# Sums of weight blocks made by adding transfers, loads begun earlier, and a new order of seven products

## The chip, the cores and the metric

The kernel runs on one core of one Trainium2 chip. The metric is the device time in microseconds (us), as the median of several executions. One more execution was profiled; all rows below come from it.

## The reference, cut to what matters

Two layers of a decoder trunk on 256 tokens of width 1024. Each layer is an FFN, a token mixer and a second FFN, each with a residual:

```
x = x + 0.5 * swiglu(rms(x), w_up, w_down)     # four times in all
x = x + mixer(rms(x))                          # delta/retention heads, then dilated/differential attention

def swiglu(h, w_up, w_down):                   # w_up: 1024 x 5632, w_down: 2816 x 1024
    gate, up = split(h @ w_up, 2)
    return (silu(gate) * up) @ w_down
```

All of it is float32. The change touches the four FFNs only.

## The kernel before, in words

**Numbers and products.** Each float32 weight block `w` is split into `hi` (ScalarE, line 219) and `lo = w - hi` (VectorE, called DVE, line 220), and each product is made of three matmuls on TensorE (PE): lines 321, 322 and 323. Blocks are 128 x 1024 elements, 512 KB.

**The stream.** `stream` lists all weight blocks in the order in which PE uses them. `block()` hands out the next one and keeps four more in preparation (`LOOKAHEAD`), by calling `feed()`, which issues the load of a plain block into a `w` tile on the queue of SP (line 218, five buffers) and emits lines 219 and 220 into five `hi` and five `lo` buffers.

**The up half of an FFN.** The 2816 columns are done in six chunks (0 to 4 of 512 columns, 5 of 256), each for gate and for up. Chunk 0 and chunk 5 are plain: 8 and 4 blocks of 12 matmuls. Chunks 1 and 2, and 3 and 4, form pairs (`seven_and`): the second of a pair (`mate`) is plain, with blocks G0 to G3 and U0 to U3, and for the first a 2 x 2 block product of Strassen's kind with seven products P1 to P7 replaces the eight (gate and up columns against the two halves of the contraction). Let W00, W01, W10, W11 be the four quarters of the weight: first index the half of the rows, second gate or up. Each quarter comes in two blocks (p = 0, 1). The sums of weights are:

```
a = W00 (P1)          t = W00 + W01 (P5)      d = W11 (P3)
u = t + W11 (P6)      b = W01 + W11 (P7)      c = W10 (P2)      u + W10 (P4)
```

A product block takes 6 matmuls. The raw quarters and the sums live in tiles with the tag `raw`, ten buffers (`RAW_BUFS`), and so does `xf`, two tiles that `sums` needs while it makes the sums of the inputs (`forms`: `keep`, then `fhP` and `flP`, lines 404, 411, 275, 276). In `form` the DVE makes t, u, b and u + W10 by adds of 128 x 1024 (line 180).

**The down half.** `seven_down` makes the product of the first eight row blocks for both column halves in the same way, mixed with the plain blocks H0 to H6; seven plain blocks for the second half follow. Here the loads are `early`: begun eight blocks ahead in place of four, and t and b are made by two transfers into the same tile, the second of them with `accum_op=ALU.add`, issued by GpSimd (POOL, line 172). u and u + W10 are made by DVE.

**What sets the order.** Each engine works through its own queue in order. The instructions are put on the queues ahead of time by a scheduler that mostly follows the order in which they are written. A tile of a tag waits until one of its buffers is free. Small steps of other work (`sums`, `turn`) are mixed in by `tick()` after each block.

Of the kernel before, what the change touches and what calls it, by code (L numbers as in the profile page):

```python
# [15 lines left out]
ALU = mybir.AluOpType  # L16
# [9 lines left out]
KF = FF // P  # L26
# [6 lines left out]
W_BUFS = 5  # L33
S_BUFS = 5
LOOKAHEAD = 4
LEAD, EARLY, RAW_BUFS = 4, 8, 10
GDN_STEPS, RET_STEPS, GDN_LAG = 2, 3, 2
LAMBDA_INIT = 0.8 - 0.6 * math.exp(-0.3)
BIG = 1.0e30
# [6 lines left out]
def trunk(ctx, tc, a, out):  # L46
# [34 lines left out]
                r.append((kk, n, pieces))  # L81
        return r

    SEVEN = ("P1", "G0", "G1", "P6", "G2", "G3", "P7", "U0", "U1", "P5", "U2", "U3", "P2", "P4", "P3")

    DOWN = ("H0", "H1", "P1", "H2", "P6", "H3", "P7", "H4", "P5", "P2", "H5", "P4", "P3", "H6")

    def one(w, k0, nk, c, n=CW):
        return (k0, nk, n, [(w, c, n)])

    def seven(w, cols, n, order, early=False, **between):

        kb = BLK // n

        def quarter(i, j, p):
            r0 = (4 * i + kb * p) * P
            return w[r0:r0 + kb * P, cols[j]:cols[j] + n].rearrange("(k p) c -> p k c", p=P)

        st = {}
        r = []  # L100
        for x in order:
            if x[0] == "P":
                r += [(x, p, st, quarter, n, early) for p in range(4 // kb)]
            else:
                r.append(between[x[0]][int(x[1])])
        return r
# [21 lines left out]

    def down_runs(w):

        return seven(w, (0, CW), CW, DOWN, True, H=cut([one(w, 8, KF - 8, 0)])) + cut([one(w, 8, KF - 8, CW)])

    def in0_runs(w):
        r = [one(w, 0, 8, 512), one(w, 0, 8, 0), one(w, 0, 8, 2048, 264), one(w, 0, 8, 1024),
# [7 lines left out]
    def out_runs(w, first):  # L142
        return [one(w, k0, 4, c * CW) for k0 in (first, 4 - first) for c in (0, 1)]

    stream = (up_runs(a["l0_ffn1_w_up"], True) + down_runs(a["l0_ffn1_w_down"])
              + cut(in0_runs(a["l0_w_in"]) + out_runs(a["l0_w_out"], 4))
              + up_runs(a["l0_ffn2_w_up"]) + down_runs(a["l0_ffn2_w_down"])
              + up_runs(a["l1_ffn1_w_up"]) + down_runs(a["l1_ffn1_w_down"])
              + cut(in1_runs(a["l1_w_in"]) + out_runs(a["l1_w_out"], 4))
              + up_runs(a["l1_ffn2_w_up"]) + down_runs(a["l1_ffn2_w_down"]))  # L150

    ready = []
    pos = [0, 0]
# [1 line left out]
    spool = [None]  # L155
    loaded = [0]

    def load(x, p, st, quarter, n, early):

        def raw(nm):  # L160
            if nm not in st:
                st[nm] = spool[0].tile([P, BLK], F32, tag="raw", name="raw", bufs=RAW_BUFS)
            return st[nm]

        if early:

            for nm, *src in {"P1": (("a", (0, 0)),), "P6": (("t", (0, 1), (0, 0)), ("d", (1, 1))),
                             "P7": (("b", (0, 1), (1, 1)),), "P2": (("c", (1, 0)),)}.get(x, ()):
                v = raw(nm + str(p)).rearrange("p (k n) -> p k n", n=n)
                nc.sync.dma_start(out=v, in_=quarter(*src[0], p))  # L170
                if src[1:]:
                    nc.gpsimd.dma_start(out=v, in_=quarter(*src[1], p), accum_op=ALU.add)
            return
        for nm, i, j in {"P1": (("a", 0, 0),), "P6": (("b", 0, 1), ("d", 1, 1)), "P2": (("c", 1, 0),)}.get(x, ()):
            nc.sync.dma_start(out=raw(nm + str(p)).rearrange("p (k n) -> p k n", n=n), in_=quarter(i, j, p))

    def form(x, p, st, early):

        def add(out, in0, in1):
            nc.vector.tensor_tensor(out=out, in0=in0, in1=in1, op=ALU.add)  # L180

        def new():
            return spool[0].tile([P, BLK], F32, tag="raw", name="raw", bufs=RAW_BUFS)

        g = {k[0]: v for k, v in st.items() if k[1] == str(p)}
        if x == "P6":
            if not early:
                st[f"t{p}"] = g["t"] = new()
                add(g["t"], g["a"], g["b"])
            st[f"u{p}"] = g["u"] = new()  # L190
            add(g["u"], g["t"], g["d"])
        elif x == "P7" and not early:
            add(g["b"], g["b"], g["d"])
        elif x == "P4":
            add(g["u"], g["u"], g["c"])
        return g[{"P1": "a", "P6": "u", "P7": "b", "P5": "t", "P2": "c", "P4": "u", "P3": "d"}[x]]

    def feed():
        i = pos[1]
        while loaded[0] < len(stream) and loaded[0] <= i + (EARLY if stream[loaded[0]][-1] is True else LEAD):  # L200
            if isinstance(stream[loaded[0]][0], str):
                if spool[0] is None:
                    break
                load(*stream[loaded[0]])
            loaded[0] += 1
        pos[1] += 1
        hi = wpool.tile([P, BLK], F32R, tag="hi", name=f"hi{i}", bufs=S_BUFS)
        lo = wpool.tile([P, BLK], F32R, tag="lo", name=f"lo{i}", bufs=S_BUFS)
        if isinstance(stream[i][0], str):
            n = stream[i][4]  # L210
            k = BLK // n
            w = form(*stream[i][:3], stream[i][5])
        else:
            k, n, pieces = stream[i]
            w = wpool.tile([P, BLK], F32, tag="w", name=f"w{i}", bufs=W_BUFS)
            wv = w[:, :k * n].rearrange("p (k n) -> p k n", n=n)
            for at, m, src in pieces:
                nc.sync.dma_start(out=wv[:, :, at:at + m], in_=src)
        nc.scalar.copy(out=hi[:, :k * n], in_=w[:, :k * n])  # L219
        nc.vector.tensor_tensor(out=lo[:, :k * n], in0=w[:, :k * n], in1=hi[:, :k * n].bitcast(F32), op=ALU.subtract)  # L220
        ready.append((k, hi[:, :k * n].rearrange("p (k n) -> p k n", n=n),
                      lo[:, :k * n].rearrange("p (k n) -> p k n", n=n)))

# [165 lines left out]
    def ffn(n, nxt):  # L389
        with tc.tile_pool(name="gpool", bufs=1) as gpool:  # L390
# [5 lines left out]
            def sums(src_hi, src_lo):  # L396
# [9 lines left out]
                    yield  # L406
                q = {(i, t): xf[i][:, :, t * P:(t + 1) * P] for i in range(2) for t in range(NT)}
                keep = gpool.tile([P, 4, P], F32, tag="post", name="keep", bufs=4)
                for nm, i0, i1, op in (("P7", q[0, 0], q[0, 1], ALU.subtract), ("P5", q[0, 1], q[1, 1], ALU.subtract),
                                       ("P6", None, q[0, 0], ALU.subtract), ("P3", None, q[1, 0], ALU.add)):  # L410
                    nc.vector.tensor_tensor(out=keep, in0=keep if i0 is None else i0, in1=i1, op=op)
                    hi = gpool.tile([P, 4, P], F32R, tag="fh" + nm, name="fh" + nm)
                    lo = gpool.tile([P, 4, P], F32R, tag="fl" + nm, name="fl" + nm)
                    split(hi, lo, keep)
                    forms[nm] = (hi, lo)
                    yield
# [44 lines left out]
            def seven_and(c, mate):  # L461


                pa, pb, pc, pd = pA("p1"), pB("p6"), pA("p5"), pA("p7")
                gate = [pA("gate"), pB("gate")]
                product("P1", pa)
                q = post("q")
                nc.scalar.copy(out=q, in_=pa)
                xs_run(gate, xT_hi, xT_lo, 0, 4)
                product("P6", pb)  # L470
                tt(q, q, pb)
                xs_run(gate, xT_hi, xT_lo, 4, 4)
                s2 = [silu(gate[t], t) for t in range(NT)]
                product("P7", pd)
                r = post("r")
                tt(r, q, pd)
                up = [pB("up"), pA("up")]
                xs_run(up, xT_hi, xT_lo, 0, 4)
                product("P5", pc)
                tt(r, pc, r, ALU.subtract)  # L480
                xs_run(up, xT_hi, xT_lo, 4, 4)
                next(spawn(turn(mate, [times(up[t], s2[t], t) for t in range(NT)], CW)))
                product("P2", pa, True)
                s0 = silu(pa, 0)
                product("P4", pd, True)
                g1 = post("g1")
                tt(g1, q, pd)
                s1 = silu(g1, 1)
                product("P3", pc, True)
                tt(q, pc, q, ALU.subtract)  # L490
                next(spawn(turn(c, [times(q, s0, 0), times(r, s1, 1)], CW)))

            spool[0] = gpool
            c = 0
# [17 lines left out]
            def seven_down(y):  # L512
# [19 lines left out]
                product("P6", pb)  # L532
                tt(q, q, pb)
                rest(1)
                product("P7", pd)
                r = post("r")
                tt(r, q, pd)
                rest(1)
                into(1, 0, q, 0.5)
                into(0, 1, q, -0.5)  # L540
                product("P5", pc)
                tt(r, pc, r, ALU.subtract)
                product("P2", pa, True)
                into(0, 0, pa, 0.5)
                rest(1)
                into(1, 1, r, 0.5)
                product("P4", pd, True)
                into(1, 0, pd, 0.5)
                product("P3", pc, True)
                into(0, 1, pc, 0.5)  # L550
                rest(1)

            for hf in range(2):
# [8 lines left out]
                g = spawn(half_done(y, hf, 0.5, nxt))  # L562
                next(g, None)
            spool[0] = None

    def out_proj(oT_hi, oT_lo, nxt, first, need):
        ys = [[pA(f"y{h}") for _ in range(NT)] for h in range(2)]
# [759 lines left out]
```

## Time and profile before

| | us |
|---|---|
| three timed runs, median | 1010.08 |
| lowest, highest | 1007.51, 1011.33 |
| profiled execution, its own time | 1007.63 |
| its span, first to last instruction | 1005.8 |
| PE busy | 985.9 (98%) |
| DVE busy | 880.1 (88%) |

The span is what the profile shows from the first to the last instruction; the time of the execution has 1.8 us more around it. PE matmuls are pipelined, so that one of 390 ns starts every 227 ns; busy shares of PE are high whatever it does, and starts are the better measure.

### The profile page before, as it was taken

The numbers are of one execution on the slowest core, as the hardware profiler recorded it, in microseconds if no ns is written. First come the engines' busy times: TensorE is split into PE (matmuls) and PEld (weight loads), VectorE is DVE, ScalarE is ACT, GpSimd is POOL, SyncE is SP. The second block draws the span as 40 slices with busy tenths as digits, with TensorE's granted clock in tenths as the row PEclk, the third lists the DMA queues.
The fourth block names the chain that finished last, engine by engine and source line by source line (L and its number), as shares of the span: only waits on it lengthen the run. The fifth ranks groups of instructions, "written<-read, shape, count | busy, mean of one in ns | idle before, by whom it ended". The sixth has DMA issues, their size and how long they took to land.

```text
span 1005.8 us, 13951 instructions
## 1 busy us (share of the span) xinstructions
PE 985.9 (98%) x5076; PEld 812.9 (81%) x5076; DVE 880.1 (88%) x1191; ACT 609.0 (61%) x829; POOL 48.9 (5%) x56
## 2 busy tenths in 40 slices
PE   7999999999999999999999999999999999999997
PEld 6788878888777888888788888878877888888785
DVE  6999999679997699999979899998679879999994
ACT  6576666579543566666656566656556556666562
POOL 0000100100001000000000000100100000001000
PEclk9999999999999999999999999999999999999999
DMA  9665963765403577499267747935752566749731
GB/s 321 228 228 180 291 200 128 238 171 149 141 12 110 156 259 245 124 277 267 84 212 270 248 144 241 292 101 188 232 168 88 167 210 209 248 150 289 230 106 62
DMA packets 104708, 192.69 MB, mean 192 GB/s; under 512 B 6560, under 2 KB 16944, under 8 KB 104640
## 3 DMA queue, kind: packets, MB, share of 16 engines
q1 hardware_dynamic: 98752, 179.89, 55.1%
q0 software_dynamic: 5312, 11.30, 5.6%
q8 instruction: 40, 0.66, 0.3%
q10 hardware_dynamic: 576, 0.61, 0.2%
q14 instruction: 28, 0.23, 0.1%
HBM read 190.73 MB, written 1.05 MB: 191 GB/s over the span
## 4 chain that ended last, share of the span: by engine, by line
PE 89%; DVE 5%; ACT 2%; issue 1%; DMA 1%; POOL 1%; SPq 0%; POOLq 0%; ACTq 0%; DVEq 0%
PE p L322 7%; PE p L323 7%; PE p L321 7%; PE y L321 6%; PE y L323 6%; PE y L322 6%; PE gate L323 6%; PE gate L321 6%; PE gate L322 6%; PE up L321 4%; PE up L322 4%; PE up L323 4%; PE ca L321 2%; PE ca L322 2%; PE ca L323 2%; PE gtr L452 2%
## 5 line engine op out<-in xcount | busy, mean ns | idle before, releaser
L220 DVE TENSOR_TENSOR lo<-w,hi 128x1024 fp32r<-128x1024 f32 (+2 forms) x238 | 284.5, 1210 | 65.0 <-ACT hi L219 64.6
L219 ACT CAST hi<-w 128x1024 fp32r<-128x1024 f32 (+2 forms) x238 | 245.5, 1044 | 128.7 <-PE y L323 50.7
L219 ACT CAST hi<-raw 128x1024 fp32r<-128x1024 f32 x168 | 174.4, 1053 | 132.2 <-DVE raw L180 49.5
L220 DVE TENSOR_TENSOR lo<-raw,hi 128x1024 fp32r<-128x1024 f32 x168 | 201.6, 1218 | 15.4 <-ACT hi L219 14.0
L321 PE MATMUL gate<-hi,xT_hi 128*128 128x512 f32 x256 | 101.3, 400 | 2.1 <-ACT xT_hi L278 1.9
L323 PE MATMUL gate<-hi,xT_lo 128*128 128x512 f32 x256 | 101.0, 395 | 0.0
L322 PE MATMUL gate<-lo,xT_hi 128*128 128x512 f32 x256 | 100.7, 393 | 0.0
L180 DVE TENSOR_TENSOR raw<-raw 128x1024 f32<-128x1024 f32 x80 | 97.0, 1216 | 0.3
L321 PE MATMUL y<-hi,gT_hi 128*128 128x512 f32 x224 | 87.2, 392 | 1.8 <-ACT hi L219 1.8
L323 PE MATMUL y<-hi,gT_lo 128*128 128x512 f32 x224 | 87.4, 390 | 0.0
L322 PE MATMUL y<-lo,gT_hi 128*128 128x512 f32 x224 | 87.2, 389 | 0.0
L321 PE MATMUL p<-hi,fhP 128*128 128x512 f32 x192 | 75.2, 392 | 0.2
L322 PE MATMUL p<-lo,fhP 128*128 128x512 f32 x192 | 74.9, 390 | 0.1
L323 PE MATMUL p<-hi,flP 128*128 128x512 f32 x192 | 74.7, 389 | 0.0
L321 PE MATMUL up<-hi,xT_hi 128*128 128x512 f32 x192 | 74.7, 389 | 0.0
L322 PE MATMUL up<-lo,xT_hi 128*128 128x512 f32 x192 | 74.7, 389 | 0.0
L323 PE MATMUL up<-hi,xT_lo 128*128 128x512 f32 x192 | 74.7, 389 | 0.0
L321 PEld LDWEIGHTS gate<-hi,xT_hi 128*128 128x128 f32 x256 | 48.5, 190 | 12.3 <-ACT xT_hi L278 2.3
L323 PEld LDWEIGHTS gate<-hi,xT_lo 128*128 128x128 f32 x256 | 48.6, 190 | 10.3
L322 PEld LDWEIGHTS gate<-lo,xT_hi 128*128 128x128 f32 x256 | 48.7, 190 | 9.7
L321 PEld LDWEIGHTS y<-hi,gT_hi 128*128 128x128 f32 x224 | 41.7, 188 | 11.2 <-ACT hi L219 3.0
L323 PEld LDWEIGHTS y<-hi,gT_lo 128*128 128x128 f32 x224 | 42.1, 188 | 8.7
(322 smaller groups left out, 1868.0 us busy)
## 6 DMA issues: line engine op xcount, KB each, us to landing
w<-l_ffn_w_up SPq DMA_DIRECT2D x95, 512.0 KB, 4.2
raw<-l_ffn_w_up SPq DMA_DIRECT2D x64, 512.0 KB, 4.9
w<-l_ffn_w_down SPq DMA_DIRECT2D x56, 512.0 KB, 5.1
w<-l_w_in SPq DMA_DIRECT2D x50, 512.0 KB, 3.8
raw<-l_ffn_w_down SPq DMA_DIRECT2D x40, 512.0 KB, 6.5
w<-l_ffn_w_up SPq DMA_DIRECT2D x34, 256.0 KB, 4.8
raw<-l_ffn_w_down POOLq DMA_DIRECT2D x16, 512.0 KB, 9.9
w<-l_w_out SPq DMA_DIRECT2D x16, 512.0 KB, 3.6
```

The costliest lines, as they stand in the source:

```text
L180: nc.vector.tensor_tensor(out=out, in0=in0, in1=in1, op=ALU.add)
L219: nc.scalar.copy(out=hi[:, :k * n], in_=w[:, :k * n])
L220: nc.vector.tensor_tensor(out=lo[:, :k * n], in0=w[:, :k * n], in1=hi[:, :k * n].bitcast(F32), op=ALU.subtract)
L321: nc.tensor.matmul(ps, lhsT=xh, rhs=wh, start=start, stop=False, skip_group_check=more)
L322: nc.tensor.matmul(ps, lhsT=xh, rhs=wl, start=False, stop=False, skip_group_check=more)
L323: nc.tensor.matmul(ps, lhsT=xl, rhs=wh, start=False, stop=stop, skip_group_check=more)
L452: nc.tensor.transpose(ps[:, j * P:(j + 1) * P], gs[t][:, j * P:(j + 1) * P], ident)
```

## The change

Up and down parts now share one way of loading and one order of products. t and b are made by adding transfers in all parts. After `hi` and `lo` of P6 are made from u, an adding transfer from GpSimd puts W10 on top of u, and P4 takes it as it is. u itself is still an add of DVE (t + d). Loads of raw blocks begin eight blocks ahead everywhere, at most two stream entries of that kind in one `feed`, after the `w` load of that `feed` and not before it, and none of the next FFN's before it has begun. The order of products is P1, P6, P5, P3, P7, P2, P4; the input sums are made in the order P5, P6, P3, P7, and the code that combines the products follows: `r = P5 - q`, then `u0 = P3 - q`, then `r = r - P7`, then P2, and at last `q = q + P4` (P2 still adds onto P1's bank, P3 onto P5's, P4 onto P7's).

```
-LEAD, EARLY, RAW_BUFS = 4, 8, 10
+LEAD, RAW_BUFS = 8, 10
-    SEVEN = ("P1", "G0", "G1", "P6", "G2", "G3", "P7", "U0", "U1", "P5", "U2", "U3", "P2", "P4", "P3")
+    SEVEN = ("P1", "G0", "G1", "P6", "G2", "G3", "P5", "U0", "U1", "P3", "P7", "U2", "U3", "P2", "P4")
-    DOWN = ("H0", "H1", "P1", "H2", "P6", "H3", "P7", "H4", "P5", "P2", "H5", "P4", "P3", "H6")
+    DOWN = ("H0", "H1", "P1", "H2", "P6", "H3", "P5", "H4", "P3", "P7", "H5", "P2", "P4", "H6")
...
     def load(x, p, st, quarter, n):
-        if early:
...
-        for nm, i, j in {"P1": (("a", 0, 0),), "P6": (("b", 0, 1), ("d", 1, 1)), "P2": (("c", 1, 0),)}.get(x, ()):
-            nc.sync.dma_start(out=raw(nm + str(p)).rearrange("p (k n) -> p k n", n=n), in_=quarter(i, j, p))
+        for nm, *src in {"P1": (("a", (0, 0)),), "P6": (("t", (0, 1), (0, 0)), ("d", (1, 1))),
+                         "P7": (("b", (0, 1), (1, 1)),), "P2": (("c", (1, 0)),)}.get(x, ()):
+            v = raw(nm + str(p)).rearrange("p (k n) -> p k n", n=n)
+            nc.sync.dma_start(out=v, in_=quarter(*src[0], p))
+            if src[1:]:
+                nc.gpsimd.dma_start(out=v, in_=quarter(*src[1], p), accum_op=ALU.add)
...
         if x == "P6":
-            if not early:
-                st[f"t{p}"] = g["t"] = new()
-                add(g["t"], g["a"], g["b"])
             st[f"u{p}"] = g["u"] = new()
-            add(g["u"], g["t"], g["d"])
-        elif x == "P7" and not early:
-            add(g["b"], g["b"], g["d"])
-        elif x == "P4":
-            add(g["u"], g["u"], g["c"])
+            nc.vector.tensor_tensor(out=g["u"], in0=g["t"], in1=g["d"], op=ALU.add)
...
     def feed():
-        while loaded[0] < len(stream) and loaded[0] <= i + (EARLY if stream[loaded[0]][-1] is True else LEAD):
...
+        some = 0
+        while loaded[0] < len(stream) and loaded[0] <= i + LEAD:
+            if isinstance(stream[loaded[0]][0], str):
+                if spool[0] is None or loaded[0] >= ends[0] or some == 2:
+                    break
+                some += 1
+                load(*stream[loaded[0]])
+            loaded[0] += 1
...
+        if stream[i][0] == "P6":
+            nc.gpsimd.dma_start(out=w.rearrange("p (k n) -> p k n", n=n), in_=stream[i][3](1, 0, stream[i][1]),
+                                accum_op=ALU.add)
```

## Rows read from the trace of the kernel before

**Rows 1.** The page, busy times, and busy tenths in 40 slices

```profile
PE 985.9 (98%) x5076; PEld 812.9 (81%) x5076; DVE 880.1 (88%) x1191; ACT 609.0 (61%) x829; POOL 48.9 (5%) x56
...
DVE  6999999679997699999979899998679879999994
```

**Rows 2.** Timeline of PE, second FFN (start us, us, instruction), and the chain

```profile
350.04 0.39 PE L321 MATMUL gate<-hi,xT_hi 128*128 128x512 f32 x1
...
352.53 0.40 PE L323 MATMUL gate<-hi,xT_lo 128*128 128x512 f32 x1
...
375.61 0.87 PE gtr L452 x8
```

**Rows 3.** Second FFN (length; busy PE, PEld, DVE, ACT, POOL; clock; DMA; GB/s)

```profile
350.04:528.40 178.36, 177.86 (x813) 147.20 (x812) 165.31 (x183) 110.70 (x136) 6.47 (x5) 1.00 0.67 210
```

**Rows 4.** Waits of PE in all (us in total, times, longest)

```profile
PE y L321 <- ACT hi L219: 1.8, 4, 0.4
```

**Rows 5.** Timeline of PE at the start of a down half, second FFN

```profile
482.27 0.39 PE L323 MATMUL p<-hi,flP 128*128 128x512 f32 x1
...
483.65 0.73 PE L321 MATMUL y<-hi,gT_hi 128*128 128x512 f32 x2 [0.44 <-ACT hi L219]
...
484.23 0.39 PE L322 MATMUL p<-lo,fhP 128*128 128x512 f32 x1
```

**Rows 6.** Timeline of DVE and ScalarE at the same place

```profile
477.48 0.68 DVE L411 TENSOR_TENSOR keep<-keep,xf 128x512 f32<-128x512 f32 x1
...
479.57 0.69 DVE L411 TENSOR_TENSOR keep<-keep,xf 128x512 f32<-128x512 f32 x1
...
480.29 1.23 DVE L180 TENSOR_TENSOR raw<-raw 128x1024 f32<-128x1024 f32 x1
...
481.61 1.05 ACT L219 CAST hi<-raw 128x1024 fp32r<-128x1024 f32 x1 [0.69 <-DVE raw L180]
```

**Rows 7.** Waits of SP's queue

```profile
SPq L170 <- DVE keep L411: 20.3, 4, 5.1
```

**Rows 8.** The chain in the first FFN (start us, us, what)

```profile
37.87 2.27 DVE raw L180 x2
```

**Rows 9.** Timeline of PE there

```profile
44.55 0.39 PE L321 MATMUL p<-hi,fhP 128*128 128x512 f32 x1
...
46.27 0.39 PE L323 MATMUL p<-hi,flP 128*128 128x512 f32 x1
```

**Rows 10.** Line 180 over the span (duration ns min/median/max)

```profile
L180 DVE TENSOR_TENSOR raw<-raw x80: 1208/1215/1226, 33.6 to 968.5; 128x1024 f32<-128x1024 f32 x80
```

**Rows 11.** Two saturated stretches: plain loads alone, and both kinds

```profile
8.00:14.00 6.00, 5.57 (x14) 4.31 (x15) 5.21 (x8) 5.17 (x13) 0.00 (x0) 1.00 1.05 406
...
642.00:646.00 4.00, 4.00 (x23) 3.38 (x22) 4.00 (x6) 2.02 (x3) 0.00 (x0) 1.00 1.10 263
```

**Rows 12.** The first pair of the second FFN as a stretch

```profile
372.73:415.50 42.77, 42.77 (x198) 35.59 (x197) 40.60 (x42) 27.20 (x31) 0.00 (x0) 1.00 0.59 196
```

**Rows 13.** Line 172 over the span (ns min/median/max), and us to landing

```profile
L172 POOL DMA_DIRECT2D raw<-l_ffn_w_down x16: 1195/1197/1402, 106.4 to 927.7; - x16
...
DMA to landing us min/median/max: 6.3/9.9/11.9
```

**Rows 14.** DMA issues (KB each, median us to landing)

```profile
raw<-l_ffn_w_up SPq DMA_DIRECT2D x64, 512.0 KB, 4.9
```

**Rows 15.** Timeline of DVE in the first pair of the second FFN

```profile
375.46 3.49 DVE L180 TENSOR_TENSOR raw<-raw 128x1024 f32<-128x1024 f32 x3
...
380.12 1.23 DVE L220 TENSOR_TENSOR lo<-raw,hi 128x1024 fp32r<-128x1024 f32 x1
```

**Rows 16.** Timeline of PE and DVE around a read of P6

```profile
427.37 0.39 PE L323 MATMUL p<-hi,flP 128*128 128x512 f32 x1
...
429.28 1.22 DVE L180 TENSOR_TENSOR raw<-raw 128x1024 f32<-128x1024 f32 x1
...
430.41 0.68 DVE L432 TENSOR_TENSOR q<-q,p 128x512 f32<-128x512 f32 x1
```

More of the change, by code (lines that the diff above doesn't have):

```diff
@@ L82, in cut, with seven @@
         return r
-    SEVEN = ("P1", "G0", "G1", "P6", "G2", "G3", "P7", "U0", "U1", "P5", "U2", "U3", "P2", "P4", "P3")
-    DOWN = ("H0", "H1", "P1", "H2", "P6", "H3", "P7", "H4", "P5", "P2", "H5", "P4", "P3", "H6")
+    SEVEN = ("P1", "G0", "G1", "P6", "G2", "G3", "P5", "U0", "U1", "P3", "P7", "U2", "U3", "P2", "P4")
+    DOWN = ("H0", "H1", "P1", "H2", "P6", "H3", "P5", "H4", "P3", "P7", "H5", "P2", "P4", "H6")
     def one(w, k0, nk, c, n=CW):
         return (k0, nk, n, [(w, c, n)])
-    def seven(w, cols, n, order, early=False, **between):
+    def seven(w, cols, n, order, **between):
         kb = BLK // n
@@ L102, in seven @@
             if x[0] == "P":
-                r += [(x, p, st, quarter, n, early) for p in range(4 // kb)]
+                r += [(x, p, st, quarter, n) for p in range(4 // kb)]
             else:
@@ L129, in down_runs @@
     def down_runs(w):
-        return seven(w, (0, CW), CW, DOWN, True, H=cut([one(w, 8, KF - 8, 0)])) + cut([one(w, 8, KF - 8, CW)])
+        return seven(w, (0, CW), CW, DOWN, H=cut([one(w, 8, KF - 8, 0)])) + cut([one(w, 8, KF - 8, CW)])
     def in0_runs(w):
@@ L143, in out_runs @@
         return [one(w, k0, 4, c * CW) for k0 in (first, 4 - first) for c in (0, 1)]
[L145 to L150, printed above, removed]
+    stream, ends = [], []
+    for l, w_in, w_out, in_runs, out_first in ((0, a["l0_w_in"], a["l0_w_out"], in0_runs, 4),
+                                               (1, a["l1_w_in"], a["l1_w_out"], in1_runs, 4)):
+        for f in (1, 2):
+            stream += up_runs(a[f"l{l}_ffn{f}_w_up"], not stream) + down_runs(a[f"l{l}_ffn{f}_w_down"])
+            ends.append(len(stream))
+            if f == 1:
+                stream += cut(in_runs(w_in) + out_runs(w_out, out_first))
     ready = []
@@ L156, in trunk, with load @@
     loaded = [0]
-    def load(x, p, st, quarter, n, early):
+    def load(x, p, st, quarter, n):
         def raw(nm):
@@ L163, in raw, with form @@
             return st[nm]
-        if early:
[L167 to L173, printed above, removed]
-        for nm, i, j in {"P1": (("a", 0, 0),), "P6": (("b", 0, 1), ("d", 1, 1)), "P2": (("c", 1, 0),)}.get(x, ()):
-            nc.sync.dma_start(out=raw(nm + str(p)).rearrange("p (k n) -> p k n", n=n), in_=quarter(i, j, p))
-    def form(x, p, st, early):
-        def add(out, in0, in1):
-            nc.vector.tensor_tensor(out=out, in0=in0, in1=in1, op=ALU.add)
+        for nm, *src in {"P1": (("a", (0, 0)),), "P6": (("t", (0, 1), (0, 0)), ("d", (1, 1))),
[4 more added lines that the diff above has]
+                nc.gpsimd.dma_start(out=v, in_=quarter(*src[1], p), accum_op=ALU.add)
+    def form(x, p, st):
         def new():
@@ L199, in feed @@
         i = pos[1]
-        while loaded[0] < len(stream) and loaded[0] <= i + (EARLY if stream[loaded[0]][-1] is True else LEAD):
[L201 to L205, printed above, removed]
         pos[1] += 1
@@ L208, in feed @@
         lo = wpool.tile([P, BLK], F32R, tag="lo", name=f"lo{i}", bufs=S_BUFS)
[L209 to L213, printed above, removed]
+        w = None
+        if not isinstance(stream[i][0], str):
             k, n, pieces = stream[i]
@@ L218, in feed @@
                 nc.sync.dma_start(out=wv[:, :, at:at + m], in_=src)
+        some = 0
[6 more added lines that the diff above has]
+            loaded[0] += 1
+        if w is None:
+            n = stream[i][4]
+            k = BLK // n
+            w = form(*stream[i][:3])
         nc.scalar.copy(out=hi[:, :k * n], in_=w[:, :k * n])
         nc.vector.tensor_tensor(out=lo[:, :k * n], in0=w[:, :k * n], in1=hi[:, :k * n].bitcast(F32), op=ALU.subtract)
+        if stream[i][0] == "P6":
+            nc.gpsimd.dma_start(out=w.rearrange("p (k n) -> p k n", n=n), in_=stream[i][3](1, 0, stream[i][1]),
+                                accum_op=ALU.add)
         ready.append((k, hi[:, :k * n].rearrange("p (k n) -> p k n", n=n),
@@ L408, in sums @@
                 keep = gpool.tile([P, 4, P], F32, tag="post", name="keep", bufs=4)
-                for nm, i0, i1, op in (("P7", q[0, 0], q[0, 1], ALU.subtract), ("P5", q[0, 1], q[1, 1], ALU.subtract),
-                                       ("P6", None, q[0, 0], ALU.subtract), ("P3", None, q[1, 0], ALU.add)):
+                for nm, i0, i1, op in (("P5", q[0, 1], q[1, 1], ALU.subtract), ("P6", None, q[0, 0], ALU.subtract),
+                                       ("P3", None, q[1, 0], ALU.add), ("P7", q[0, 0], q[0, 1], ALU.subtract)):
                     nc.vector.tensor_tensor(out=keep, in0=keep if i0 is None else i0, in1=i1, op=op)
@@ L473, in seven_and @@
                 s2 = [silu(gate[t], t) for t in range(NT)]
-                product("P7", pd)
+                product("P5", pc)
                 r = post("r")
-                tt(r, q, pd)
+                tt(r, pc, q, ALU.subtract)
                 up = [pB("up"), pA("up")]
                 xs_run(up, xT_hi, xT_lo, 0, 4)
-                product("P5", pc)
-                tt(r, pc, r, ALU.subtract)
+                product("P3", pc, True)
+                u0 = post("u0")
+                tt(u0, pc, q, ALU.subtract)
+                product("P7", pd)
+                tt(r, r, pd, ALU.subtract)
                 xs_run(up, xT_hi, xT_lo, 4, 4)
@@ L483, in seven_and @@
                 product("P2", pa, True)
-                s0 = silu(pa, 0)
+                g0 = times(u0, silu(pa, 0), 0)
                 product("P4", pd, True)
[L486 to L491, printed above, removed]
+                tt(q, q, pd)
+                next(spawn(turn(c, [g0, times(r, silu(q, 1), 1)], CW)))
             spool[0] = gpool
@@ L534, in seven_down @@
                 rest(1)
[L535 to L538, printed above, removed]
                 into(1, 0, q, 0.5)
@@ L541, in seven_down @@
                 product("P5", pc)
-                tt(r, pc, r, ALU.subtract)
+                r = post("r")
+                tt(r, pc, q, ALU.subtract)
+                rest(1)
+                product("P3", pc, True)
+                into(0, 1, pc, 0.5)
+                product("P7", pd)
+                tt(r, r, pd, ALU.subtract)
+                into(1, 1, r, 0.5)
+                rest(1)
                 product("P2", pa, True)
                 into(0, 0, pa, 0.5)
-                rest(1)
-                into(1, 1, r, 0.5)
                 product("P4", pd, True)
                 into(1, 0, pd, 0.5)
-                product("P3", pc, True)
-                into(0, 1, pc, 0.5)
                 rest(1)
@@ L564, in ffn @@
             spool[0] = None
+            ends.pop(0)
     def out_proj(oT_hi, oT_lo, nxt, first, need):
```

## Prediction

> **What bounds the kernel now.** I read the busy times and the slices first, then the pitch of the matmuls, then every place where the pitch breaks, and last the DMA rows, because the change moves work from VectorE (DVE) onto the DMA engines. The page shows PE busy for 98% of the span and DVE for 88%, with DVE at nine tenths in many slices [rows 1]. A busy share says little for a pipelined PE, so I count starts. In the second FFN the matmul of 512 columns that starts at 350.04 us is followed by eleven more by 352.53 us: (352.53 - 350.04) / 11 = 0.2265 us each [rows 2]. One FFN has 756 such matmuls: 504 in the up half (96 for chunk 0, 180 for each of two pairs, 48 for the last chunk) and 252 in the down half. 756 x 0.2265 = 171.2 us, and 60 transposes at 0.11 us (eight take 0.87 us on the chain [rows 2]) are 6.5 us. That is 177.7 us of a stretch that lasts 178.4 us [rows 3]. So PE is the bound and nearly seamless: a faster DVE can win only where PE actually waits. The waits of PE for ACT's `hi` are four at `y` in the down halves, 1.8 us in all [rows 4], and one at `gate` in the first FFN; around each the pitch is broken for about 1 us. So there are two kinds.
>
> The first kind stands at the start of every down half, four times. From 482.27 to 484.23 us four pitches take 1.96 us where 4 x 0.2265 = 0.91 is normal: 1.05 us lost [rows 5]. PE waits for `hi` of the second P6 block (481.61, released by the DVE add L180). That add starts at 480.29, at the moment the last `keep` of the form sums ends (479.57 + 0.69 = 480.26) [rows 6]. The add writes a new `raw` tile; `xf`, which `keep` reads, has the same tag and the same ten buffers. SP shows the same: four loads of line 170 waited for `keep` [rows 7]. So it is a wait for a buffer, not for DVE's throughput: in a down half of before, t, d, b of both halves (6), two `xf`, c and u of both halves (4) are 12 tiles for 10 buffers when P6 is formed.
>
> The second kind stands once, in the first FFN: the chain runs through adds L180, two in a row from 37.87 us [rows 8], and more DVE work up to 44 us, and PE loses (46.27 - 44.55) - 0.91 = 0.81 us [rows 9].
>
> **The change part by part.** *Removed adds.* Of 80 adds L180 [rows 10] an up part had eight (t, u, b and u+c for each half), a down part four (u, u+c). Both now keep two. Eight up parts and four down parts: 8 x 6 + 4 x 2 = 56 adds x 1.215 us = 68 us of DVE time. Their cover is PE itself: DVE is off the path in all but the places above, so I credit 0 for them except in the first FFN, where two to three of the adds between 33 and 44 us (2.4 to 3.6 us) go ahead of a 0.81 us loss: I take 0.8 us gained, bounds 0 and 0.8.
>
> *Buffers at the start of a down half.* In the new order P7 comes after P3, so its b tiles are loaded eight blocks before position 13 instead of before position 8, and no early list holds c. When the second P6 block is formed the live tiles are t, d (4), `xf` (2), b (2), u (2): ten, which just fits, and c follows at positions 8 and 9. The wait on `keep` should go: 4 x 1.05 = 4.2 us gained. Bounds: 4.2, or 0 if the order on the queues lets c take a buffer before u does. I take 4.2, since even with one c ahead u gets the `xf` that is free after the third form and not after the fourth, and that was about 2.1 us earlier (477.48 + 0.68 against 480.26) [rows 6].
>
> *Added transfers.* An up part loaded 8 blocks of w and 8 of raw, 512 KB each. Now it has 8 w, 10 plain raw and 6 adding ones (t, b and c onto u). Price of a plain one: where only SP's queue is at work and DMA is saturated, 406 GB/s, 0.524 MB / 406 = 1.29 us [rows 11]. Price of an adding one: the trace has 16. Where they meet plain loads in saturation the two together move 263 GB/s [rows 11]; a pair of one each then takes 1.049 / 263 = 3.99 us, so an adding one costs 3.99 - 1.29 = 2.70 us. The part then needs 18 x 1.29 + 6 x 2.70 = 39.4 us of DMA against 42.7 us of PE (372.73 to 415.4) [rows 12]; before it needed 16 x 1.29 = 20.6. It fits, at 92%. In chunk 0, the last chunk and the second half of the down part there is room to run ahead. Taken: 0. Its upper bound is that an adding one moves nothing beside it: 23.2 + 6 x 3.99 = 47.1 us, 4.4 us too much for each of eight parts, 35 us.
>
> *Latency of the sums.* An adding transfer lands 9.9 us after its issue (6.3 to 11.9) [rows 13]; a plain raw load 4.9 [rows 14]. P6's t: plain load, then the add, 4.9 + 9.9 = 15 us, begun eight blocks ahead of a feed that itself runs up to four blocks ahead of PE; blocks are 6 or 12 matmuls, 1.36 or 2.72 us. Ahead of the first P6 block of a second part stand six product blocks and two w blocks, 13.6 us, so 1.3 us of the four blocks of lead (5 us and more) are used up; the rest stays as reserve. The tightest is the second b, for P7. GpSimd's queue is in order, and an add of c onto u waits until `lo` of P6 is made from u. In the second FFN that `lo` of the second P6 block ends at 381.35 [rows 15]. If u1, b0 and b1 then queue up 4 us apart, they land at 391.3, 395.3 and 399.3. PE needs the second P7 block after nine product blocks and six w blocks, (54 + 72) x 0.2265 + 0.87 = 29.4 us after 372.73, at 402.1, less 2.3 us for `hi` and `lo`: 399.8. The margin is 0.5 us with the old times; of the three adds in one row at 375.46 [rows 15] two are removed, so `lo` comes about 2.4 us earlier and the margin is some 3 us. Taken: 0.
>
> *Wait for DVE's reading of a bank.* Products that share a bank wait for its reading: P3 adds into the bank of P5, and in the down half only one w block (2.72 us) stands between. The latest such read that I found starts at 430.41, 2.65 us after the product's end (427.37 + 0.39), behind an add L180 [rows 16]. With its own 0.68 us it would be 0.6 us too long for one w block: bounds 0 to 0.6 us, four times, 0 to 2.4 us. I take 0, because the adds that stood ahead of that read are the ones that go.
>
> *Start.* In the first FFN two raw loads now stand before the fourth w load. At saturation that is 2 x 1.29 = 2.6 us later for each w behind them: bounds 0 to 2.6 us. I take 0, since fewer adds wait on DVE when the blocks come in.
>
> *Queues.* On SP's queue the w load of a feed now goes ahead of the raw loads of that feed, which costs the raw loads one issue of 0.4 us and is hidden by eight blocks of lead: 0. GpSimd's other work is one `pow` per norm; should it come to stand behind an add that waits for its plain load, ACT needs it only after the eight blocks of chunk 0, 8 x 12 x 0.2265 = 21.7 us later: 0.
>
> *Sum.* -0.8 - 4.2 = -5.0 us, and I keep 0.1 to 0.5 us for small new waits: -4.7. The profiled execution took 1007.63 us (span 1005.8 and 1.8 around it): 1003 us. It lies 2.45 us under the median of the runs, 1010.08; on the median's footing the forecast is 1005.3 us, -0.47%.
>
> **The Trainium skill against the trace.** The rows show GpSimd's 16 instructions for adding transfers at 1195 to 1402 ns each, in stretches where DVE is busy nine tenths [rows 13, 1]. The Trainium skill, "SBUF — State Buffer", section "SBUF: two separate sides", says that a DMA issued from GpSimd gets its descriptors written through a port pair that DVE can lock, so that such a DMA waits while DVE operations of a two-port kind run, and gives about 620 ns alone against 3100 overlapped. [...]
>
> **The rivals.** *The adding transfers come late (slower).* The place is the second b of P7 in each of eight up parts. The margin is 0.5 to 3 us; it decides from the point where four adding transfers in a row land more than about 5 us apart, or DMA needs more than 42.7 us for a part. For it: 92% of DMA, one in-order queue on GpSimd that has to wait for u. Against it: 4 us apart is what the saturated stretches show, and buffers give lead. If it loses 2 us in each part: 8 x 2 = 16 us, 1010.08 + 16 - 5 = 1021 us; with 1 us each 1013.
>
> *Only DVE gets lighter (no change).* The wait at the down half stays or is replaced, because c or the later forms take the buffer, or P6's sums wait for their own transfer: only the 0.8 us of the first FFN is gained, 1009.3 us. For it: ten tiles for ten buffers leaves nothing over.
>
> *GpSimd starves.* If descriptors could be written only in DVE's idle time: a part would have 42.7 - (40.6 - 7.3) = 9.4 us of idle DVE, by the 40.6 us that the part has now [rows 12] less six adds, for 6 x 1.2 = 7.2 us of descriptors, fragmented; at a loss of 3 us per part, 24 us, 1029 us. I name it because of the rule of the Trainium skill's "SBUF — State Buffer" cited above.
>
> *The bank of P5 (same).* 4 x 0.6 us lost of the 5 gained: 1010.08 - 5 + 2.4 = 1007.5 us.
>
> **How the numbers follow.** What a measurement of this kernel can tell from no change is about 0.5%, 5 us; the forecast lies at this border. Forecast 0.48 (half of it over 0.5%); only DVE lighter 0.17; bank of P5 0.08; adding transfers late 0.20; starved 0.03; something freed that I don't see (over 6 us) 0.04. Faster: 0.24 + 0.04 = 0.28. Slower: 0.18 of the late case and 0.03, 0.21. Same: 0.24 + 0.17 + 0.08 + 0.02 = 0.51. The likeliest case's own range is 1002 to 1008 us. The whole range: below, the fastest run less the full gain and a little, 1007.51 - 6 = 1001; above, the late case at about 1.1 us a part, 1010.08 + 8.8 = 1019.
>
> **What would show it.** Right: 24 adds L180 left, DVE near 812 us busy; 72 adding transfers; the pitch unbroken at the start of all four down halves; no wait of SP for `keep` ahead of u; DMA near 0.9 in the up parts; adding transfers still near 10 us. Wrong: breaks of the pitch inside the up parts with ACT's `hi` waiting for a DMA; adding transfers landing after 12 us or more; u of the down half still behind `keep`.

## The result, and the profile after

The changed kernel takes 1037.28 us (median of 4 runs, 1036.11 to 1037.7) against 1008.99 for the kernel before: a ratio of 1.0275, 95% interval 1.0255 to 1.0296. The forecast was 1005.3 us, with a range up to 1019: wrong, and on the other side. The profiled execution has a span of 1034.3 us, 28.5 more than before.

The page of the kernel after (busy times; the costliest groups; DMA issues with KB each and median us to landing) answers to [rows 1, 10, 13]:

```profile
PE 994.1 (96%) x5076; PEld 818.4 (79%) x5076; DVE 822.3 (80%) x1135; ACT 615.9 (60%) x829; POOL 115.5 (11%) x112
...
L183 DVE TENSOR_TENSOR raw<-raw 128x1024 f32<-128x1024 f32 x24 | 29.3, 1221 | 28.3 <-DMA raw<-l_ffn_w_up 21.7
...
w<-l_ffn_w_up SPq DMA_DIRECT2D x95, 512.0 KB, 8.4
...
raw<-l_ffn_w_up POOLq DMA_DIRECT2D x48, 512.0 KB, 9.6
```

VectorE did get lighter (880.1 to 822.3 us busy), 24 adds are left, and the median adding transfer lands as late as forecast (9.6 us in the up parts, 9.9 forecast). But the adds that are left, now line 183 (u = t + d), had VectorE idle for 28.3 us ahead of them, 21.7 of it until a transfer landed. In the kernel before, two adds of line 180 stand at the same place of the second FFN without a wait (timeline of DVE, kernel before):

```profile
364.92 1.22 DVE L180 TENSOR_TENSOR raw<-raw 128x1024 f32<-128x1024 f32 x1
...
368.40 1.22 DVE L180 TENSOR_TENSOR raw<-raw 128x1024 f32<-128x1024 f32 x1
```

The start of the down half in the second FFN, the place of [rows 5] (timeline of PE, kernel after):

```profile
497.01 0.39 PE L316 MATMUL p<-hi,fhP 128*128 128x512 f32 x1
...
498.37 0.39 PE L316 MATMUL p<-hi,fhP 128*128 128x512 f32 x1
...
499.73 0.39 PE L316 MATMUL y<-hi,gT_hi 128*128 128x512 f32 x1
```

Both P6 blocks run without a break: twelve matmuls in 2.72 us, 0.227 each. The gain that the forecast counted on is there. The loss is elsewhere (waits of PE and of DVE in the kernel after: us in total, times, longest):

```profile
PE gtr L447 <- DVE g L436: 17.2, 6, 4.6
...
DVE raw L183 <- DMA raw<-l_ffn_w_up: 21.7, 7, 6.4
...
DVE raw L183 <- issue: 6.6, 2, 5.1
```

`gtr` are the transposes of g, the first thing that PE needs from a finished chunk. They wait for the product `g` (line 436, function `times`); in the kernel before the eight of them took 0.87 us on the chain [rows 2]. Why `g` is late shows in the same stretch of the second FFN, on GpSimd, DVE and PE (three timelines, kernel after):

```profile
367.56 1.25 POOL L173 DMA_DIRECT2D raw<-l_ffn_w_up  x1 [3.50 <-PE gate L318]
```

```profile
370.05 0.69 DVE L271 TENSOR_TENSOR flP<-keep,fhP 128x512 fp32r<-128x512 f32 x1
377.11 1.23 DVE L183 TENSOR_TENSOR raw<-raw 128x1024 f32<-128x1024 f32 x1 [6.38 <-DMA raw<-l_ffn_w_up]
378.25 0.68 DVE L406 TENSOR_TENSOR keep<-keep,xf 128x512 f32<-128x512 f32 x1
...
387.07 0.69 DVE L271 TENSOR_TENSOR flP<-keep,fhP 128x512 fp32r<-128x512 f32 x1
387.67 1.41 DVE L436 SCALAR_TENSOR_TENSOR g<-up,rstd,s 128x512 f32<-128x512 f32 x2
```

```profile
383.44 0.39 PE L318 MATMUL p<-hi,xT_lo 128*128 128x512 f32 x1
388.47 1.97 PE L447 MATMUL gtr<-ident,g 128*128 128x128 f32 x8 [4.65 <-DVE g L436]
390.09 0.78 PE L316 MATMUL gate<-hi,xT_hi 128*128 128x512 f32 x1
...
394.08 0.49 PE L316 MATMUL gate<-hi,xT_hi 128*128 128x512 f32 x1
```

t's adding transfer is issued at 367.56. From 370.7 DVE stands still until the u add can start at 377.11, 9.55 us after that issue. Eleven more instructions follow before `g` starts at 387.67, back to back: DVE has no slack left, so PE's transposes start 5.03 us after the last matmul where 0.23 is the pitch. PE does not need u before the P6 matmuls, two w blocks and eight transposes further on. It was not late for u; it was late for what stood behind u. The same break stands in the first pairs of the third and the fourth FFN (3.5 and 4.4 us from one start to the next); where the u add of a second pair stands ahead of the `g` of the first pair there are three more (3.2 and 1.8 us in the first FFN, 1.5 in the last). The u adds there have their waits put down to "issue" (5.1 and 1.5 us), but they start 8.9 and 8.3 us after the issue of an adding transfer. A late u add holds back a `lo` of line 211 as well. In the fourth FFN PE waits 1.5 us for one (timelines of DVE and of PE, kernel after), and in the first one 2.3 us at 29.38:

```profile
862.81 1.23 DVE L183 TENSOR_TENSOR raw<-raw 128x1024 f32<-128x1024 f32 x1 [1.97 <-DMA raw<-l_ffn_w_up]
863.95 1.22 DVE L211 TENSOR_TENSOR lo<-raw,hi 128x1024 fp32r<-128x1024 f32 x1
```

```profile
865.22 0.50 PE L317 MATMUL p<-lo,xT_hi 128*128 128x512 f32 x1 [1.47 <-DVE lo L211]
```

The stall costs a second time (windows of the kernel after: length; busy PE, PEld, DVE, ACT, POOL; granted clock; DMA share; GB/s):

```profile
383.80:388.40 4.60, 0.02 (x1) 0.00 (x0) 4.57 (x7) 2.57 (x4) 2.39 (x2) 0.90 1.02 332
388.40:394.00 5.60, 5.53 (x17) 4.76 (x18) 5.27 (x7) 2.76 (x5) 2.42 (x2) 0.50 1.05 237
```

After 4.6 us without work PE runs at a granted clock of 0.50, the lower of its two levels, 1.2 GHz. The eight transposes take 390.09 - 388.47 = 1.62 us in place of 0.87, and the nine pitches from 390.09 to 394.08 take 3.99 us in place of 9 x 0.227 = 2.04. So this one place costs 4.8 + 0.75 + 1.95 = 7.5 us.

### The profile page after: what moved, and what is told of

Same layout as the page of the kernel before. It is cut to its first block, busy times and chain, and to the rows that moved or that the text cites. A ratio compares the mean times of both kernels' runs of the same rounds, so it can differ in the third digit from the quotient of the medians.

```text
span 1034.3 us, 14154 instructions
## 1 busy us (share of the span) xinstructions
PE 994.1 (96%) x5076; PEld 818.4 (79%) x5076; DVE 822.3 (80%) x1135; ACT 615.9 (60%) x829; POOL 115.5 (11%) x112
## 4 chain that ended last, share of the span: by engine, by line
PE 75%; DVE 9%; DMA 9%; issue 3%; ACT 2%; POOL 0%; SPq 0%; POOLq 0%; DVEq 0%; ACTq 0%
DMA raw<-l_ffn_w_up 8%; PE p L316 6%; PE p L318 6%; PE y L318 6%; PE p L317 6%; PE y L316 6%; PE y L317 6%; PE gate L316 5%; PE gate L318 5%; PE gate L317 5%; DVE lo L211 3%; PE up L317 2%; PE up L318 2%; PE up L316 2%; PE ca L316 2%
## 5 line engine op out<-in xcount | busy, mean ns | idle before, releaser
L316 PE MATMUL gate<-hi,xT_hi 128*128 128x512 f32 x256 | 104.5, 409 | 1.8 <-ACT xT_hi L273 1.8
L173 POOL DMA_DIRECT2D raw<-l_ffn_w_up x32 | 38.8, 1212 | 218.5 <-DMA raw<-l_ffn_w_up 75.8
L183 DVE TENSOR_TENSOR raw<-raw 128x1024 f32<-128x1024 f32 x24 | 29.3, 1221 | 28.3 <-DMA raw<-l_ffn_w_up 21.7
```

The lines of the kernel that those rows point to most:

```text
L183: nc.vector.tensor_tensor(out=g["u"], in0=g["t"], in1=g["d"], op=ALU.add)
L316: nc.tensor.matmul(ps, lhsT=xh, rhs=wh, start=start, stop=False, skip_group_check=more)
```

## The experiments

Theory A: the u add, early in VectorE's in-order queue, waits for t's adding transfer and holds `g` back. Theory B: the volume of the transfers does it. Theory C: a sum is too late for PE itself. Each ratio is against the kernel before, run beside it; its median moved between 1007.65 and 1009.84 us, so runs are compared by their ratios.

**Run 1: the u add queued behind g** (`times` keeps its last instruction in `last_g`).

```
+            with tc.issue_after(last_g[0]):
                 nc.vector.tensor_tensor(out=g["u"], in0=g["t"], in1=g["d"], op=ALU.add)
```

> All transfers stay as in the changed kernel; the add u = t + d is only queued on VectorE behind the latest product g = up * s that the program has written before it. Theory A (the u add stands early in VectorE's in-order queue, waits there for t's adding transfer, and keeps g, the transposes behind it and so TensorE waiting): the six waits of the transposes for g (17 to 20 us together) and the half-speed matmuls behind them (about 6 us) go, and the time falls from 1037.3 to 1008-1016 us. Theory B (the transfers' volume: 72 adding transfers delay the loads of w and the sums whatever the order): the time stays within 3 us of 1037. Theory C (the sum u is too late for TensorE itself): the wait moves from g to the first matmul of P6 and the time stays above 1030.

Measured: 1016.36 us, ratio 1.009 (1.0065 to 1.0115). About 19 us of 28 are back (1.0275 - 1.009 = 0.0185) with every transfer in place; the time lies 0.4 us above A's range. No u add waits for a transfer, and the wait of `gtr` falls from 17.2 to 1.7 us. B and C are out as the main cause.

**Run 2: the wait taken away, the add still ahead of g.** P6 and P4 of the up parts are then products of another sum; the transfers are all there.

```
-  in0=g["t"], in1=g["d"]
+  in0=g["a" if "_u" in st else "t"], in1=g["d"]      # "_u": an up part
```

> All transfers and the places in the queues stay, but in the up parts u is made from a and d instead of t and d, so that the add waits for plain loads alone (P6 and P4 of these parts are then products of another sum). Theory A: like the kernel with the forced order, 1008-1016 us, although the u add still stands ahead of g. Theory B (volume): above 1033, since not one transfer is less. If only the place in the queue mattered and not the wait for t's transfer, it would stay at 1037 too.

Measured: 1005.6 us, ratio 0.9977 (0.9968 to 0.9987): 30 us less than the changed kernel (1.0275 - 0.9977 = 0.0298), and the figure of the forecast itself. The u add stands ahead of `g`, even three instructions further forward than in the changed kernel (right behind the second `xf`), and waits 0.16 us; the DMA engines are busier than in the changed kernel (a share of 1.07 against 1.02 in its own first pair, 380.94 to 423.00) and PE is busy without a gap (timeline of DVE, then the stretch of the first pair; columns as above):

```profile
361.98 1.23 DVE L183 TENSOR_TENSOR raw<-raw 128x1024 f32<-128x1024 f32 x1 [0.16 <-DMA raw<-l_ffn_w_up]
...
374.87 1.40 DVE L437 SCALAR_TENSOR_TENSOR g<-up,rstd,s 128x512 f32<-128x512 f32 x2
```

```profile
372.00:415.00 43.00, 43.00 (x199) 35.83 (x198) 34.57 (x36) 26.71 (x30) 7.25 (x6) 1.00 1.07 318
```

So it is the wait for t's transfer, not a place ahead of `g` and not the bytes.

**Run 3: t first.** In the up parts t's two transfers go with P1's block, ahead of a.

```
-  "P1": (("a", (0, 0)),), "P6": (("t", (0, 1), (0, 0)), ("d", (1, 1))),
+  "P1": (("t", (0, 1), (0, 0)), ("a", (0, 0))), "P6": (("d", (1, 1)),),
```

> As the changed kernel, but in the up parts the plain load and the adding transfer of t are issued with P1's block and ahead of a, instead of with P6's block behind both a. Every transfer and every add stays, and the u add stays ahead of g. Theory A: t lands about 3 us earlier at the start of each FFN, so each of the four long waits of the transposes for g shrinks by about 3 us, and the time falls to 1018-1028 us. Theory B: no byte less, the time stays above 1033.

Measured: 1026.57 us, 1.0174 (1.0152 to 1.0196), in A's range. The mechanism in detail was not as expected (timeline of DVE):

```profile
371.68 1.23 DVE L185 TENSOR_TENSOR raw<-raw 128x1024 f32<-128x1024 f32 x1 [6.47 <-DMA raw<-l_ffn_w_up]
```

The wait is as long as before (6.47 us), because the add now stands still earlier in the queue, right behind the second `xf`. But it ends 7.7 us after the start of that `xf` (363.99 here), and in the changed kernel 10.1 us after it (367.05): 2.4 us earlier, and less is lost at `gtr` (13.6 us in all in place of 17.2). That is 3.6 of the 10 us that the run gains; the rest was not placed.

**Runs 4 and 5: one sum back on VectorE, the wrong one and the right one.** Run 4 makes b there, run 5 makes t.

```
run 4, up parts:  b loaded plain from W01;  at P7:  b = b + d  on VectorE
run 5, up parts:  t loaded plain from W01;  at P6:  t = a + t  on VectorE
```

> As the changed kernel, with only b of the up parts made by VectorE from plain loads (one adding transfer of three less in each up part's sums of two sources; the u add stays where it was). Theory A: the u add still waits for t's adding transfer ahead of g, so the time stays at 1030-1040 us. Theory B (volume): with 16 adding transfers out of 72 gone, about a fifth of the loss of 28 us goes or more: 1020-1032. Theory C' (b is the late sum): 1010-1020.

> In the up parts alone t is again a sum that VectorE makes (W01 loaded plain into t's tile, then t = a + t); b and the c onto u stay adding transfers, and so does everything in the down parts; order and lead are those of the changed kernel. Theory A: the u add then waits for plain loads, which land about 10 us earlier, so the waits for g go: 1008-1016 us. Theory B: the same bytes are asked for in the same stretch up to one tile in five of the part, so the time stays above 1030. A rival within A, that the later adding transfers (b, c onto u) cost too: 1017-1028.

Run 4: 1033.52 us, 1.0241 (1.0222 to 1.026), as A has it; b alone was not the trouble. Run 5 is a miss: 1059.46 us, 1.0509 (1.0487 to 1.0531), slower than the changed kernel. Ahead of the second FFN's first pair the add of t now waits 1.2 us only, but that of the second pair's t (line 185 there), fed in the middle of the first pair, waits long (timeline of DVE; waits of PE):

```profile
411.82 1.21 DVE L215 TENSOR_TENSOR lo<-raw,hi 128x1024 fp32r<-128x1024 f32 x1
419.31 1.22 DVE L185 TENSOR_TENSOR raw<-raw 128x1024 f32<-128x1024 f32 x1 [6.28 <-DMA raw<-l_ffn_w_up]
```

```profile
PE gtr L451 <- DVE g L440: 17.0, 14, 4.1
PE p L321 <- DVE lo L215: 12.1, 7, 3.5
```

The same head of the queue in another place: a plain load can hold it as well as an adding one. That its load came late because a holds its buffer until t is made is argued, not shown.

**Runs 6 to 8: the 11 us that run 1 leaves above run 2.** In its second pairs run 1 shows the place of the rival *The adding transfers come late* (its timelines of GpSimd, where line 216 is c onto u and 174 is b, and of ACT, the casts of b):

```profile
429.71 2.44 POOL L216 DMA_DIRECT2D raw<-l_ffn_w_up  x2 [16.86 <-DMA raw<-l_ffn_w_up]
431.57 3.07 POOL L174 DMA_DIRECT2D raw<-l_ffn_w_up  x2
```

```profile
445.26 1.05 ACT L212 CAST hi<-raw 128x1024 fp32r<-128x1024 f32 x1 [3.51 <-DMA raw<-l_ffn_w_up]
449.17 1.05 ACT L212 CAST hi<-raw 128x1024 fp32r<-128x1024 f32 x1 [2.87 <-DMA raw<-l_ffn_w_up]
```

With u made late, c onto u and b stand together in GpSimd's queue, b last. Run 6 adds b on VectorE (run 4's edit) to run 1; run 7 frees the down parts from the forced order; run 8 does both.

```
run 7:  with tc.issue_after(last_g[0]) if "_u" in st else ExitStack():
```

> The kernel with the u add queued behind g (1016.4 us), and in the up parts b = W01 + W11 made by VectorE from plain loads instead of an adding transfer; t and the c onto u stay transfers. That kernel is 10.8 us above the one whose u add waits for plain loads alone; there, in the second pairs, the casts of b wait 2.9 and 3.5 us for its adding transfer and TensorE breaks its pitch at P7. If b's late transfer is that rest: 1005-1010 us. If the rest is the transfers' volume or the lateness of u itself: 1013-1018.

> The u add queued behind g in the up parts alone; in the down parts it is free again. With the order forced everywhere the down parts show a break of 1.34 us in each of the four FFNs, with half-speed matmuls behind, 5.4 us in all, which the changed kernel does not have. If those come from the forced order in the down parts: 1010-1013 us, 5 us under the kernel with the order forced everywhere. If they come from the up parts' transfers, pushed later: 1015-1018.

> The same, and b of the up parts made by VectorE from plain loads. If the late b of the second pairs is what is left of the loss (2.9 and 3.5 us of waits of its casts there): 1005-1009 us, level with the kernel whose u add waits for plain loads alone. If not: within 1.5 us of the kernel with b by transfers.

Run 6: 1013.37 us, 1.0038 (1.002 to 1.0055). In us that is the lower edge of the second expectation, which said that b is not the rest; but the kernel before was 2.2 us slower beside it than beside run 1. By the ratios 0.0052 of run 1's excess of 0.0113 over run 2 is gone: the late b was about half of the rest. Run 7 is a miss, 1030.74 us, 1.0202 (1.0161 to 1.0243). Its profile shows the theory once more, in the part where the add was set free (timelines of GpSimd and DVE, the next down part's t and u; then waits of PE):

```profile
458.19 1.21 POOL L174 DMA_DIRECT2D raw<-l_ffn_w_down  x1 [21.77 <-DMA raw<-l_ffn_w_down]
```

```profile
467.33 1.22 DVE L185 TENSOR_TENSOR raw<-raw 128x1024 f32<-128x1024 f32 x1 [2.55 <-issue]
...
476.60 0.74 DVE L438 SCALAR_TENSOR_TENSOR g<-r,rstd,s 128x512 f32<-128x512 f32 x1
```

```profile
PE gtr L449 <- DVE g L438: 14.2, 9, 4.0
```

The releaser reads "issue" there, but the add starts 9.1 us after the issue of the transfer that it needs, and the transposes of this `g` wait 3.99 us. That b's late transfers push the down part's t back is argued, not shown. Run 8, where they are gone, takes 1006.8 us, 0.9971 (0.9954 to 0.9988), level with run 2. Against run 6 it gains 0.0067, 6.8 us: the price of the order forced in the down parts, where run 6 has four waits of `y` for `hi`, 3.8 us in all, and run 8 none.

**Run 9: the start.** Run 8, with the raw loads four blocks ahead while the first eight blocks are fed.

```
-  while loaded[0] < len(stream) and loaded[0] <= i + LEAD:
+  while loaded[0] < len(stream) and loaded[0] <= i + (4 if i < 8 else LEAD):
```

> As the kernel with the u add queued behind g in the up parts and b made by VectorE there (1006.8 us), but while the first eight blocks of the program are fed the raw loads run four blocks ahead, as in the kernel before, instead of eight. In that kernel the first seven-product matmul of the first FFN starts at 38.1 us; in the kernel before at 34.1. Theory S (four raw loads stand ahead of the fourth to sixth load of w at the start): that matmul starts at 34-35.5 us and the time falls by 2.5-4 us, to 1003-1004.5. Rival (the late matmul comes from the adding transfers' bytes or from VectorE's order): 37-38 us, and 1006-1007.5.

Measured: 1003.31 us, 0.9944 (0.9928 to 0.9961). SP's queue in run 8, then in run 9:

```profile
4.45 1.32 SPq L174 DMA_DIRECT2D raw<-l_ffn_w_up  x2
5.81 2.03 SPq L203 DMA_DIRECT2D w<-l_ffn_w_up  x3
7.88 1.36 SPq L174 DMA_DIRECT2D raw<-l_ffn_w_up  x2
9.88 0.56 SPq L203 DMA_DIRECT2D w<-l_ffn_w_up  x1
11.12 1.64 SPq L174 DMA_DIRECT2D raw<-l_ffn_w_up  x2
13.72 8.45 SPq L203 DMA_DIRECT2D w<-l_ffn_w_up  x4
```

```profile
8.52 6.38 SPq L203 DMA_DIRECT2D w<-l_ffn_w_up  x3
14.95 2.71 SPq L174 DMA_DIRECT2D raw<-l_ffn_w_up  x5
```

The first seven-product matmul starts at 38.12 us in run 8 and at 32.91 in run 9 (34.11 in the kernel before). Theory S holds, its gain of 3.5 us inside the range (2.7 by the ratios, whose intervals overlap), its start 1.1 us earlier than expected. Its count of the loads was rough: in run 8 two raw loads stand ahead of the fourth `w` load, four ahead of the seventh and six ahead of the eighth.

**Runs 10 to 12: parts of the change alone.** Run 10 leaves the up parts as before (plain loads, four sums on VectorE, four blocks ahead) and keeps the new order and the new down parts. Run 11 adds the c onto u by transfer to it, run 12 also the second source of b, onto b, issued when t = a + b is made.

```
run 10:  "P1": (("a", (0, 0)),), "P6": (("b", (0, 1)), ("d", (1, 1))), "P2": (("c", (1, 0)),)   # all plain
         at P6:  t = a + b;  u = t + d     at P7:  b = b + d     at P4:  u = u + c
run 11:  as 10, c onto u by nc.gpsimd.dma_start(..., accum_op=ALU.add)
run 12:  as 11, and after t = a + b:  W11 onto b by nc.gpsimd.dma_start(..., accum_op=ALU.add)
```

> The up parts load plain and make all four sums on VectorE as in the kernel before, four blocks ahead; only the order of the products and what was done to the down parts (order, c onto u by a transfer) is left of the change. If the gain at the start of the down parts that the forecast counted is real and the new order of products costs nothing: 1003.5-1006.5 us, about 4 us under the kernel before. If the order itself (P5 P3 P7, two waits for a bank) costs in the up parts: 1008-1012. If the gain in the down half of the changed kernel came from its lighter up parts: within 1.5 us of the kernel before.

> As the kernel with the up parts of before (1003.3 us), but the c onto u of the up parts by an adding transfer, so that VectorE makes three sums of four there and waits for plain loads alone. Nothing on VectorE's queue waits for that transfer: only the casts of P4, ten blocks later. Theory A: the same time within 1.5 us, 1002-1005, since VectorE's own time is not what ends the waits. If VectorE's load still bounds the up parts: 1000-1002. If an adding transfer costs by its volume: 1006-1010.

> As the kernel with three sums on VectorE and c onto u by a transfer (1003.8 us), but b's second source too comes onto b by an adding transfer, issued when VectorE has formed t = a + b. So two sums of four are transfers, and t and u, the two that VectorE's queue has ahead of g, wait for plain loads alone. Theory A: no loss, 1002-1006 us. If the transfer of b is late for P7's casts, some 25 us after t is formed: a break of pitch at P7 and 1008-1014. If adding transfers cost by their number: 1007-1012 (halfway to the forced order).

Measured: 1003.34 us, 0.9956 (0.994 to 0.9972); 1003.83 us, 0.995 (0.9935 to 0.9965); 1004.64 us, 0.9947 (0.9924 to 0.997). The three and run 9 lie within each other's intervals, and all beat both kernels by intervals below 1. VectorE is busy 872.4 us in run 10 and 838.9 in run 12: 34 us that nobody waits for. What decides is not how many sums are transfers but which: c and b's second half have no reader on VectorE ahead of `g`; t has one.

## Why the prediction was wrong

**The step that failed** is *Latency of the sums*, in its part on P6's t: "the rest stays as reserve ... Taken: 0". It measured t's 15 us against the moment at which PE needs P6. The reader of t that counts is the u add, which stands on VectorE ahead of the form sums and of `g`. The rule of asking what is queued behind a waiting instruction was applied to GpSimd's queue and not to this one. The adding transfer itself was sized well (the add starts 9.55 us after the issue, 9.9 taken); the moment of need was wrong, and it was worked out for a second part alone, while most of the loss stands in first pairs. By run 2 the term is 30 us, not 0. The profile after bears the size out: beyond the pitch the six late starts of the transposes lose 4.8 + 3.3 + 4.2 + 3.0 + 1.5 + 1.3 = 18.1 us, and half speed behind the three in first pairs 2.7 + 3.0 + 1.6 = 7.3 us, 25.4 us in all. Most of the rest stands at the late `lo`: 1.5 us in the fourth FFN, and a first seven-product matmul 1.7 us later than in run 2 (39.52 against 37.87). The Trainium skill, "PSUM — Partial Sum Buffer", section "Engine vs sequencer instructions", says that VectorE's queue is strictly first in, first out; the trace agrees: 6.38 us in which nothing behind the add starts.

**The start** was the second error: 0 taken, bounds 0 to 2.6 us. Up to six raw loads stand ahead of the later w loads, not two; run 9 against run 8 gives 3.5 us by the medians, 2.7 by the ratios, and the matmul 5.2 us later. The break of 0.81 us at the first P6 is gone in the changed kernel, as credited: its pitch is unbroken from 48.60 to 78 us.

**What was right.** The wait for a buffer at the start of the down half: 4.2 us forecast, 4.4 measured (run 10, 1 - 0.9956 = 0.0044), and none of the four breaks is left. The removed adds are worth nothing where PE does not wait. The bank of P5: no wait of PE for its reading in the profile after. The starved rival: GpSimd's 72 instructions for adding transfers take 1195 to 1393 ns each, as its 16 did before, so GpSimd does not starve. Volume: 92% of the DMA engines was too low, 1.07 in run 2, but 0 was the right price, since PE has no gap there. Together, without the wait: -4.4 + 2.7 = -1.7 us against run 2's -2.3; with the 30 us, which are run 2's own, +28.3 against 27.7 by the ratio.

**The rivals.** The late case ended on the right side by the wrong place. Its own place, the second b, shows no wait of PE in the changed kernel and comes up in run 1, when u is made late: there the casts of b wait 2.9 and 3.5 us, and about half of 11 us goes with b's transfer.

## What to carry to other kernels

When a sum moves from an engine to a slower transfer, look for the first reader of the result on an in-order queue, not for the engine that bounds the kernel, and price the wait by what stands behind that reader. Move first those sums whose result is read late, and count PE's half-speed restart with each stall of several us. A lead in blocks is worth nothing at the start, where the loads that run ahead push back the ones that are needed first.

## What the runs showed of the hardware

Run 2's DMA share stood at 1.07 and 318 GB/s over 43 us with six adding transfers among the loads, and PE had no gap; I had taken 263 GB/s for the two kinds together from a stretch of 4 us [rows 11]. A stall of 4.6 us put PE at a granted clock of 0.50 for the 5.6 us after it, which added half as much again to the stall's own price (2.7 us to 4.8); behind the stalls of the third and the fourth FFN it was 3.0 and 1.6 us.
